# A decoder block on one core: where the pooling's first differences, its weights' splits and some later low parts are made

## The chip, the cores and the metric

One NeuronCore of one Trainium2 chip runs the kernel; the other cores are idle. The metric is the device time of one execution in microseconds, the median of several runs. The engines are named as in the profile: PE is TensorE (PEld its weight loads), DVE is VectorE, ACT is ScalarE, POOL is GpSimd, SP is the engine whose queue issues most DMAs.

## What is computed

One decoder layer on a sequence of 1024 tokens with 1024 channels, in float32. Of it, what matters here (shortened):

```python
h = rms_norm(x, norm_gain) * (1.0 + scale) + shift
q, k, v, z_a, u, z_b, m_a, m_b = split(h @ w_in)           # eight blocks of 1024 columns
p_a = (stick_breaking_attention(q, k, v) * silu(z_a)) @ w_branch_a
# pooling: four groups of 256 channels, trailing windows 2, 4, 8, 16
d = (trailing mean of u over the window) - u               # divided by the available count
pooled = (d @ pool_w[group]) * pool_scale
p_b = (pooled * silu(z_b)) @ w_branch_b
out = x + gate * ((sigmoid(m_a) * p_a + sigmoid(m_b) * p_b) @ w_out)
return rms_norm(out, final_gain)
```

## The kernel before

**Products in two parts.** A float32 operand of a matmul is split into a high part (a cast to the type fp32r, which TensorE takes at full rate) and a low part (the rest, original minus high part). Each product is made from three matmuls: high with high, high with low, low with high (`mm3`, line 152). A matmul has 128 rows of weights and 512 columns. So every weight tile of 128x1024 costs a DMA of 512 KB, a cast and a subtraction of 1024 columns per partition: `split` (line 103) takes the engine of the cast and that of the subtraction as arguments, `load_w` (line 118) loads into the tag `raw` (two buffers, pool `wts`) and splits into the tag `whl` (two buffers).

**Low parts made ahead.** The attention's 40 weight tiles take their low parts from DRAM, except the first eight (`PLAIN`). `make_lo` (line 131) makes them in stages in which there is room: it loads a tile (`l_raw`), ScalarE casts it (`l_hi`), VectorE subtracts in place, and it is stored to `wl_d`. Eight are made beside the product u, fourteen beside v (`LO_V`, 7 in each half), ten after the tiles of pb (`LO_PB`), in program order. Their buffers: three for `l_raw` and one for `l_hi`, in the pool that is open (`vp`, then `pb`).

**Stages, in order.** (1) Loads, norm, modulation, transposition of x into hT, and the product u for the first 512 tokens. (2) u for the rest; its tiles go to DRAM (`u_d`). The weights of u lie in the pool `first`, opened ahead of `init` on the left side of SBUF and closed after v. (3) The values v (lines 353 to 373): 16 tiles of 24 matmuls in two halves; each is emptied from its PSUM bank by a cast on ScalarE and a subtraction on VectorE and stored to `v_d`. (4) The pooling (lines 377 to 425), in pool `pb`: per group of 256 channels two differences, each of a load of u, one to four adds of 1024 columns (tag `win`), a subtraction (`d`, line 397) with two short instructions for its first tokens, and a split into the tag `dhl` (three buffers), all on VectorE; the group's pool weights (`praw`, in the tag `raw` of `wts`; split into `phl`, one buffer); then two output tiles, each with the projection `wzb` (48 matmuls, its weights cast by VectorE and their low part made by GpSimd), the silu of it (lines 409 to 411), twelve matmuls of the pooled tile into the PSUM tag `tr`, and a scaling out of the bank (line 423), a cast and a subtraction into `gb`. (5) pb (lines 428 to 442): gb times w_branch_b, eight weight tiles split by VectorE and GpSimd, with the gate's sum `gacc` beside it. (6) The attention, interleaved with its projections. Its pool `atz` is on the right side of SBUF; `kl` is set to zero by GpSimd at its start (line 460). (7) The attention's output product, the final product and norm.

**What sets the order.** The framework traces the program and then orders each engine's instructions by a simulated timeline, in which an instruction goes as soon as its inputs and its buffer are there, the earlier one in the program first. Only what is pinned keeps its program order: the matmuls and transpositions of stages 1 and 6 and a few loads and casts. In stages 2 to 5 nothing is pinned, so a step can be placed far ahead of or behind its place in the program; what holds it is its inputs and its buffer. The order so planned is fixed on every engine and queue: an instruction whose input is late holds up those behind it. A pool's memory may be that of a closed one; then a tile waits until the tiles that lay there are no longer in use.

Of the kernel before, what the change touches and what calls it, by code (L numbers as in the profile page):

```python
# [9 lines left out]
F32 = mybir.dt.float32  # L10
F32R = mybir.dt.float32r
AF = mybir.ActivationFunctionType
ALU = mybir.AluOpType
PSUM = bass.MemoryType.PSUM

P = 128
D = 1024
# [19 lines left out]
PLAIN = 8  # L37
LO_V = (1, 1, 1, 1, 1, 1, 1, 0)
LO_PB = (1, 1, 1, 1, 1, 1, 2, 2)
HD = 64  # L40

LOAD_WO = (0, 0, 0, 1, 1, 2, 2, 2)
# [8 lines left out]
def block_kernel(ctx, tc, a, out):  # L51
# [3 lines left out]
    def pool(name, **kw):  # L55
        return tc.tile_pool(name=name, bufs=1, reuse_waits="tile", **kw)
# [46 lines left out]
    def split(src, shape, pl, tag, bufs, hi_eng, lo_eng, name):  # L103
        hl = pl.tile([shape[0], 2] + list(shape[1:]), F32R, tag=tag, bufs=bufs, name=name)
        hi, lo = hl[:, 0], hl[:, 1]
        copy_to(hi_eng, hi, src)
        lo_eng.tensor_tensor(lo, src, hi.bitcast(F32), op=ALU.subtract)
        return hi, lo
# [19 lines left out]
    tiles += gates  # L128
    early_lo = iter(range(PLAIN, len(tiles)))

    def make_lo(pl, n):

        for _ in range(n):
            i = next(early_lo)
            raw = pl.tile([P, D], F32, tag="lraw", bufs=3, name=f"l{i}_raw")
            nc.sync.dma_start(raw, a["w_in"][tiles[i]])
            hi = pl.tile([P, D], F32R, tag="lhi", bufs=1, name=f"l{i}_hi")
            act.copy(hi, raw)
            v.tensor_sub(raw.bitcast(F32R), raw, hi.bitcast(F32))
            nc.sync.dma_start(wl_d[i], raw)  # L140
# [27 lines left out]
    def project(ct, name, use, he, le):  # L168
        whl = load_w(a["w_in"][ct], name, he, le)
        for sh in range(2):  # L170
            ps = bank("pj", f"{name}_{sh}")
            mm3(ps, whl, (h_hi, h_lo), range(KB), hmov(sh))
            use(sh, ps)
# [14 lines left out]


    early = ExitStack()  # L190
    first = early.enter_context(pool("first"))
    with pool("init") as init:
        sig = const.tile([P, 8], F32, name="csig")
        act.activation(sig, c_v, AF.Sigmoid)
# [143 lines left out]
            make_h(1, kb, v)  # L338


    with pool("vp") as vp:
        def load_wv(hf, k2):
            raw = wts.tile([P, 2, 512], F32, tag="raw", bufs=2, name=f"wv{hf}_{k2}_raw")
            nc.sync.dma_start(raw.rearrange("p k c -> p (k c)"), a["w_v"][hf, k2])
            return split(raw, [P, 2, 512], vp, "wv", 6, act, v, f"wv{hf}_{k2}")

        wv = [[load_wv(0, k2) for k2 in range(4)]]
        for i in reversed(range(KB)):
            ps = bank("pj", f"u{i}_1")
            mm3(ps, whl[i], h, range(KB), hmov(1))  # L350
            use[i](1, ps)
            make_lo(vp, 1)
        for hf in range(2):
            if hf == 0:
                wv.append([load_wv(1, k2) for k2 in range(4)])
            for sb in range(8):
                ss = slice(sb * P, (sb + 1) * P)
                ps = bank("pj", f"v{sb}_{hf}")
                for kb in range(KB):
                    hh, hl = h_hi[:, kb, ss], h_lo[:, kb, ss]  # L360
                    wh, wl = (w[:, kb % 2] for w in wv[hf][kb // 2])
                    for n, (l, w) in enumerate(((hh, wh), (hh, wl), (hl, wh))):
                        mm(ps, l, w, start=kb == 0 and n == 0, stop=kb == KB - 1 and n == 2)

                vo = vp.tile([P, 8, 2, HD], F32R, tag="vo", bufs=3, name=f"vo{sb}_{hf}")
                pv = ps.rearrange("p (h d) -> p h d", d=HD)
                act.copy(vo[:, :, 0], pv)
                v.tensor_sub(vo[:, :, 1], pv, vo[:, :, 0].bitcast(F32))
                nc.sync.dma_start(
                    v_d[4 * hf:4 * hf + 4, :, sb].rearrange("n p c -> p n c"),  # L370
                    vo.rearrange("p (n h) i d -> p n (h i d)", h=2).bitcast(F32),
                )
                make_lo(vp, LO_V[sb])
    early.close()


    with pool("pb") as pb:
        invn = pb.tile([P, 16], F32, name="invn")
        for j in range(16):
            gp.memset(invn[:, j:j + 1], 1.0 / (16 - j))  # L380
        gb = pb.tile([P, 2, KB, S], F32R, name="gb")
        for g, win in enumerate(WINDOWS):
            dhl = []
            for cb in range(2):
                j = 2 * g + cb
                u = pb.tile([P, S + 16], F32, tag="u", bufs=2, name=f"u{j}")
                v.memset(u[:, S:], 0.0)
                nc.sync.dma_start(u[:, :S], u_d[j])
                cur, n, step = u, S + 16, 1
                while step < win:  # L390
                    nxt = pb.tile([P, S + 16], F32, tag="win", bufs=2, name=f"win{j}_{step}")
                    n -= step
                    v.tensor_add(nxt[:, :n], cur[:, :n], cur[:, step:step + n])  # L393
                    cur, step = nxt, 2 * step
                t0 = S - win + 1
                d = pb.tile([P, S], F32, tag="win", bufs=2, name=f"d{j}")
                v.scalar_tensor_tensor(d[:, :t0], cur[:, :t0], 1.0 / win, u[:, :t0], ALU.mult, ALU.subtract)
                tl = pb.tile([P, 16], F32, tag="tl", bufs=2, name=f"tl{j}")
                v.tensor_mul(tl[:, :win - 1], cur[:, t0:S], invn[:, 16 - win + 1:])
                v.tensor_sub(d[:, t0:], tl[:, :win - 1], u[:, t0:S])  # L400
                dhl.append(split(d, [P, S], pb, "dhl", 3, v, v, f"dhl{j}"))
            praw = wts.tile([P, 2, 256], F32, tag="raw", bufs=2, name=f"praw{g}")
            nc.sync.dma_start(praw, a["pool_w"][g].rearrange("(k p) d -> p k d", p=P))
            ph, pl_ = split(praw, [P, 2, 256], pb, "phl", 1, v, v, f"phl{g}")
            for ob in range(2):
                j = 2 * g + ob
                zs = [pb.tile([P, 512], F32, tag="zs", bufs=3, name=f"zs{j}_{sh}") for sh in range(2)]

                def silu(sh, ps):
                    act.activation(zs[sh], ps, AF.Sigmoid)  # L410
                    v.tensor_mul(zs[sh], ps, zs[sh])  # L411

                project(CZB + j, f"wzb{j}", silu, v, gp)
                for sh in range(2):
                    sl = slice(sh * 512, sh * 512 + 512)
                    ps = bank("tr", f"pool{j}_{sh}")
                    for cb in range(2):
                        (dh, dl) = dhl[cb]
                        oc = slice(ob * P, ob * P + P)
                        for i, (w, m) in enumerate(((ph, dh), (ph, dl), (pl_, dh))):  # L420
                            mm(ps, w[:, cb, oc], m[:, sl], start=cb == 0 and i == 0, stop=cb == 1 and i == 2)
                    z = zs[sh]
                    v.scalar_tensor_tensor(z, ps, psc_v[:, j:j + 1], z, ALU.mult, ALU.mult)
                    act.copy(gb[:, 0, j, sl], z)
                    v.tensor_sub(gb[:, 1, j, sl], z, gb[:, 0, j, sl].bitcast(F32))
        gacc, bg = (pb.tile([P, S + 16], F32, tag="u", bufs=2, name=n)[:, :D] for n in ("gacc", "bg"))
        nc.sync.dma_start(bg, a["b_gate"].broadcast_to([P, D]))
        for j in range(KB):
            sm = [pb.tile([P, 512], F32, tag="zs", bufs=3, name=f"sm{j}_{sh}") for sh in range(2)]
            whl = load_w(a["w_branch_b"][j], f"wb{j}", v, gp)  # L430
            wg = wts.tile([P, D], F32, tag="raw", bufs=2, name=f"wg{j}")
            nc.sync.dma_start(wg, a["w_gate"][j * P:(j + 1) * P, :])
            if j == 0:
                v.tensor_scalar_mul(gacc, wg, sc[:, 0:1])
            else:
                v.scalar_tensor_tensor(gacc, wg, sc[:, j:j + 1], gacc, ALU.mult, ALU.add)
            for sh in range(2):
                ps = bank("pj", f"pb{j}_{sh}")
                mm3(ps, whl, (gb[:, 0], gb[:, 1]), range(KB), hmov(sh))
                act.copy(sm[sh], ps)  # L440
                nc.sync.dma_start(pb_d[j][:, sh * 512:sh * 512 + 512], sm[sh])
            make_lo(pb, LO_PB[j])

        for hf in range(2):
            sl = slice(hf * 512, hf * 512 + 512)
            ps = bank("z", f"gate{hf}")
            mm(ps, ones, gacc[:, sl], start=True, stop=True)
            v.tensor_add(bg[:, sl], ps, bg[:, sl])
        nc.sync.dma_start(g_d, bg[0:1, :])


    logits = ExitStack()
# [394 lines left out]
```

## Time and profile before

| | us |
|---|---|
| median of 3 runs | 1249.1 (1248.1 to 1249.2) |
| the profiled execution, its own time | 1250.9 |
| its span, first to last instruction | 1249.2 |
| PE busy | 1215.2 (97%) |
| DVE busy | 810.5 (65%) |
| ACT busy | 546.3 (44%) |
| POOL busy | 227.6 (18%) |

The chain of work that ended last is 78% PE, 10% DVE, 5% issue and 2% DMA. In the views, a row of the timeline is: start, duration, engine, line, operation, output and input, shapes, count, and in brackets the idle time of the engine before it and what ended it. Rows by stretch give the busy time of PE, PEld, DVE, ACT and POOL with counts, then the granted clock, the DMA engines' share and GB/s. Rows of groups give the count, the busy time in us and the mean in ns, and then the idle time ahead of them. A helper's line stands for all who call it: L107 and L116 are the subtraction and VectorE's cast of a split, L112 is ScalarE's, L92 every matmul.

### The profile page before, as it was taken

Reading aid. Unit: us, or ns where it says so; the run is one execution under the profiler, and the core shown is the slowest. Engines: PE = TensorE matmul, PEld = TensorE weight load, DVE = VectorE, ACT = ScalarE, POOL = GpSimd, SP = SyncE. Lnnn points to the kernel's source line nnn. Section 1 sums busy time; section 2 is a strip of 40 time slices with the busy share of each in tenths; the row PEclk is TensorE's granted clock in tenths of the full one; section 3 lists DMA queues with packets and bytes.
Section 4 is the critical chain, followed back from the end, with each engine's and each line's share of the span. In section 5 each row is a group of like instructions: output and inputs, shape, how many; then the busy total and the mean of one; then the engine's idle time right before and its main releaser. Section 6 shows DMA issues by size and latency. Waiting matters only on the chain.

```text
span 1249.2 us, 16044 instructions
## 1 busy us (share of the span) xinstructions
PE 1215.2 (97%) x5744; PEld 1005.2 (80%) x5744; DVE 810.5 (65%) x1085; ACT 546.3 (44%) x1022; POOL 227.6 (18%) x373
## 2 busy tenths in 40 slices
PE   4999999899999999999999999999999999999998
PEld 3888888688888888888888888888888888888886
DVE  6723452999511168786887877788796864685654
ACT  4654331321111256565566656566565654232101
POOL 2100010111112333221312222132222310001001
PEclk9999999989999999999999999999999999999999
DMA  8649994752344411232322333232233225985612
GB/s 325 265 151 345 320 371 163 274 202 93 118 144 135 151 52 50 69 127 90 105 89 94 114 110 111 73 121 89 89 119 110 74 89 186 352 287 170 201 65 85
DMA packets 72946, 192.97 MB, mean 154 GB/s; under 512 B 7713, under 2 KB 21025, under 8 KB 70946
## 3 DMA queue, kind: packets, MB, share of 16 engines
q1 hardware_dynamic: 62098, 172.80, 40.3%
q10 hardware_dynamic: 10768, 19.14, 4.6%
q8 instruction: 45, 0.74, 0.2%
q14 instruction: 35, 0.29, 0.1%
HBM read 137.38 MB, written 50.34 MB: 150 GB/s over the span
## 4 chain that ended last, share of the span: by engine, by line
PE 78%; DVE 10%; issue 5%; DMA 2%; POOL 1%; ACT 1%; POOLq 0%; SPq 0%; DVEq 0%; ACTq 0%
PE p L92 30%; PE pa L92 7%; PE pb L92 7%; PE v L92 7%; PE o L92 6%; PE av L92 4%; PE z L92 4%; PE u L92 4%; PE wt L92 4%; PE ua L92 2%; DVE om L583 1%; DVE be L584 1%; DMA l_raw<-in_w_in 1%; DVE win L393 1%; PE wzb L92 1%
## 5 line engine op out<-in xcount | busy, mean ns | idle before, releaser
L92 PE MATMUL p<-hT,w 128*128 128x512 f32 x1920 | 534.5, 399 | 0.0
L92 PEld LDWEIGHTS p<-hT,w 128*128 128x128 f32 x1920 | 341.5, 188 | 56.7 <-issue 0.5
L583 DVE TENSOR_TENSOR_SCAN om<-om 128x512 f32<-128x512 f32 (+7 forms) x128 | 175.2, 1368 | 51.7 <-POOL om L581 28.6
L576 ACT ACTIVATE om<-z 128x512 f32<-128x512 f32 (+2 forms) x192 | 94.3, 491 | 104.0 <-PE z L92 101.8
L603 DVE TENSOR_TENSOR wt<-wt,wt 128x512 fp32r<-128x512 f32 (+1 forms) x160 | 101.0, 632 | 47.3 <-ACT wt L602 46.0
L581 POOL TENSOR_SCALAR_AFFINE_SELECT om<-om 128x128 f32<-128x128 f32 x128 | 65.7, 514 | 328.1 <-ACT om L576 301.8
L602 ACT CAST wt<-wt 128x512 fp32r<-128x512 f32 (+1 forms) x160 | 87.3, 546 | 68.7 <-PE wt L92 65.2
L584 DVE TENSOR_TENSOR be<-be,om 128x511 f32<-128x511 f32 (+7 forms) x128 | 99.7, 779 | 10.8 <-ACT wt L602 0.5
L92 PE MATMUL av<-wt,vv 128*128 128x512 f32 x320 | 94.4, 376 | 0.0
L92 PEld LDWEIGHTS wt<-ident,be 128*128 128x128 f32 x576 | 72.0, 140 | 27.5 <-DVE wt L603 3.2
L577 ACT ACTIVATE be<-z 128x512 f32<-128x512 f32 (+2 forms) x192 | 93.6, 487 | 0.0
L92 PE MATMUL wzb<-hT,wzb 128*128 128x512 f32 x384 | 92.9, 398 | 0.1
L92 PE MATMUL wt<-ident,be 128*128 128x128 f32 x576 | 89.2, 273 | 3.8 <-DVE wt L603 3.8
L92 PE MATMUL o<-wo,mhl 128*128 128x512 f32 (+2 forms) x408 | 90.4, 380 | 0.0
L92 PE MATMUL pa<-ga,wa 128*128 128x512 f32 x384 | 89.8, 392 | 0.0
L92 PE MATMUL pb<-gb,wb 128*128 128x512 f32 x384 | 88.1, 391 | 0.0
L92 PEld LDWEIGHTS wzb<-hT,wzb 128*128 128x128 f32 x384 | 73.8, 192 | 16.8 <-DVE zs L411 0.5
L92 PE MATMUL v<-wv,hT 128*128 128x512 f32 x384 | 87.2, 389 | 0.0
L92 PEld LDWEIGHTS o<-wo,mhl 128*128 128x128 f32 x408 | 74.6, 188 | 14.4
L92 PEld LDWEIGHTS pa<-ga,wa 128*128 128x128 f32 x384 | 72.1, 188 | 15.9
L92 PEld LDWEIGHTS pb<-gb,wb 128*128 128x128 f32 x384 | 72.1, 188 | 15.8
L92 PEld LDWEIGHTS v<-wv,hT 128*128 128x128 f32 x384 | 72.1, 188 | 14.9
(121 smaller groups left out, 1458.4 us busy)
## 6 DMA issues: line engine op xcount, KB each, us to landing
w_raw<-in_w_in SPq DMA_DIRECT2D x40, 512.0 KB, 4.3
l_raw<-in_w_in SPq DMA_DIRECT2D x32, 512.0 KB, 5.8
wl_d<-l_raw SPq DMA_DIRECT2D x32, 512.0 KB, 5.3
w<-wl_d SPq DMA_DIRECT2D x32, 512.0 KB, 3.8
v_d<-vo SPq DMA_DIRECT2D x16, 512.0 KB, 5.4
vv<-v_d SPq DMA_DIRECT2D x8, 1024.0 KB, 5.8
wa_raw<-in_w_branch_a SPq DMA_DIRECT2D x16, 512.0 KB, 4.8
wa<-in_w_mod SPq DMA_DIRECT2D x7, 1024.0 KB, 8.7
```

The costliest lines, as they stand in the source:

```text
L92: ins = op(*args, **kw)
L393: v.tensor_add(nxt[:, :n], cur[:, :n], cur[:, step:step + n])
L576: act.activation(om[:, b0:b0 + n], zp[:, :n], AF.Sigmoid, scale=-0.125)
L577: act.activation(be[:, b0:b0 + n], zp[:, :n], AF.Sigmoid, scale=0.125)
L581: gp.affine_select(out=tl[:, :P], in_=tl[:, :P], pattern=[[1, P]], compare_op=ALU.is_gt, fill=fill, base=0, channel_multiplier=-1)
L583: v.tensor_tensor_scan(om[:, :W], om[:, :W], om[:, :W], 1.0, ALU.mult, ALU.min)
L584: v.tensor_mul(be[:, 1:W], be[:, 1:W], om[:, :W - 1])
L602: act.copy(wt[:, 0, :off], pt[:, :off])
L603: v.tensor_sub(wt[:, 1, :off], pt[:, :off], wt[:, 0, :off].bitcast(F32))
```

## The change

- The code of one difference becomes a function, `make_d`, with the same instructions, in a pool `dif` on the right side of SBUF. `dif` is opened after u, where `first` lay, which moves to the right side and is closed there already. The tags `u`, `win`, `tl` and `dhl` are in `dif`; `dhl` has four buffers instead of three.
- `DIFFS = {1: 0, 4: 1}`: differences 0 and 1 (the first group) stand in the program after tiles 1 and 4 of the first half of v. The others stand where they were.
- The pool weights `praw` get a tag of their own in `pb` with two buffers; `phl` has two buffers instead of one.
- The projection wzb is cast by ScalarE, and its low part is made by VectorE (before: VectorE and GpSimd).
- The ten `make_lo` after pb's tiles use buffers of the tag `dhl`, raw tile and cast side by side in one buffer. Those beside u and v are as before.
- `gacc` and `bg` take the tag `u` in `dif`; `dif` is closed after the gate. `invn` is a constant.

```diff
+DIFFS = {1: 0, 4: 1}
...
-    def make_lo(pl, n):
+    def make_lo(pl, n, tag=None):
 
         for _ in range(n):
             i = next(early_lo)
-            raw = pl.tile([P, D], F32, tag="lraw", bufs=3, name=f"l{i}_raw")
+            if tag:
+                both_ = pl.tile([P, 2, D], F32R, tag=tag, bufs=4, name=f"l{i}")
+                raw, hi = both_[:, 0].bitcast(F32), both_[:, 1]
+            else:
+                raw = pl.tile([P, D], F32, tag="lraw", bufs=3, name=f"l{i}_raw")
+                hi = pl.tile([P, D], F32R, tag="lhi", bufs=1, name=f"l{i}_hi")
             nc.sync.dma_start(raw, a["w_in"][tiles[i]])
-            hi = pl.tile([P, D], F32R, tag="lhi", bufs=1, name=f"l{i}_hi")
             act.copy(hi, raw)
             v.tensor_sub(raw.bitcast(F32R), raw, hi.bitcast(F32))
             nc.sync.dma_start(wl_d[i], raw)
...
-    first = early.enter_context(pool("first"))
+    first = early.enter_context(pool("first", side="right"))
...
+    def make_d(j):
+        win = WINDOWS[j // 2]
+        u = dif.tile([P, S + 16], F32, tag="u", bufs=2, name=f"u{j}")
+        v.memset(u[:, S:], 0.0)
+        nc.sync.dma_start(u[:, :S], u_d[j])
+        cur, n, step = u, S + 16, 1
+        while step < win:
+            nxt = dif.tile([P, S + 16], F32, tag="win", bufs=2, name=f"win{j}_{step}")
+            n -= step
+            v.tensor_add(nxt[:, :n], cur[:, :n], cur[:, step:step + n])
+            cur, step = nxt, 2 * step
+        t0 = S - win + 1
+        d = dif.tile([P, S], F32, tag="win", bufs=2, name=f"d{j}")
+        v.scalar_tensor_tensor(d[:, :t0], cur[:, :t0], 1.0 / win, u[:, :t0], ALU.mult, ALU.subtract)
...
+        dhls[j] = split(d, [P, S], dif, "dhl", 4, v, v, f"dhl{j}")
...
             use[i](1, ps)
             make_lo(vp, 1)
+        early.close()
+        diffs = ExitStack()
+        dif = diffs.enter_context(pool("dif", side="right"))
...
                 make_lo(vp, LO_V[sb])
-    early.close()
+                if 8 * hf + sb in DIFFS:
+                    make_d(DIFFS[8 * hf + sb])
...
-            praw = wts.tile([P, 2, 256], F32, tag="raw", bufs=2, name=f"praw{g}")
+            for j in (2 * g, 2 * g + 1):
+                if j not in dhls:
+                    make_d(j)
+            dhl = [dhls.pop(2 * g), dhls.pop(2 * g + 1)]
+            praw = pb.tile([P, 2, 256], F32, tag="praw", bufs=2, name=f"praw{g}")
             nc.sync.dma_start(praw, a["pool_w"][g].rearrange("(k p) d -> p k d", p=P))
-            ph, pl_ = split(praw, [P, 2, 256], pb, "phl", 1, v, v, f"phl{g}")
+            ph, pl_ = split(praw, [P, 2, 256], pb, "phl", 2, v, v, f"phl{g}")
...
-                project(CZB + j, f"wzb{j}", silu, v, gp)
+                project(CZB + j, f"wzb{j}", silu, act, v)
...
-        gacc, bg = (pb.tile([P, S + 16], F32, tag="u", bufs=2, name=n)[:, :D] for n in ("gacc", "bg"))
+        gacc, bg = (dif.tile([P, S + 16], F32, tag="u", bufs=2, name=n)[:, :D] for n in ("gacc", "bg"))
...
-            make_lo(pb, LO_PB[j])
+            make_lo(dif, LO_PB[j], "dhl")
...
+    diffs.close()
```

More of the change, by code (lines that the diff above doesn't have):

```diff
@@ L338, in block_kernel @@
             make_h(1, kb, v)
+    invn = const.tile([P, 16], F32, name="invn")
+    for j in range(16):
+        gp.memset(invn[:, j:j + 1], 1.0 / (16 - j))
+    dhls = {}
+    def make_d(j):
[12 more added lines that the diff above has]
+        v.scalar_tensor_tensor(d[:, :t0], cur[:, :t0], 1.0 / win, u[:, :t0], ALU.mult, ALU.subtract)
+        tl = dif.tile([P, 16], F32, tag="tl", bufs=2, name=f"tl{j}")
+        v.tensor_mul(tl[:, :win - 1], cur[:, t0:S], invn[:, 16 - win + 1:])
+        v.tensor_sub(d[:, t0:], tl[:, :win - 1], u[:, t0:S])
+        dhls[j] = split(d, [P, S], dif, "dhl", 4, v, v, f"dhl{j}")
     with pool("vp") as vp:
@@ L373, in block_kernel @@
                 make_lo(vp, LO_V[sb])
-    early.close()
+                if 8 * hf + sb in DIFFS:
+                    make_d(DIFFS[8 * hf + sb])
     with pool("pb") as pb:
-        invn = pb.tile([P, 16], F32, name="invn")
-        for j in range(16):
-            gp.memset(invn[:, j:j + 1], 1.0 / (16 - j))
         gb = pb.tile([P, 2, KB, S], F32R, name="gb")
         for g, win in enumerate(WINDOWS):
[L383 to L401, printed above, removed]
-            praw = wts.tile([P, 2, 256], F32, tag="raw", bufs=2, name=f"praw{g}")
+            for j in (2 * g, 2 * g + 1):
[3 more added lines that the diff above has]
+            praw = pb.tile([P, 2, 256], F32, tag="praw", bufs=2, name=f"praw{g}")
             nc.sync.dma_start(praw, a["pool_w"][g].rearrange("(k p) d -> p k d", p=P))
-            ph, pl_ = split(praw, [P, 2, 256], pb, "phl", 1, v, v, f"phl{g}")
+            ph, pl_ = split(praw, [P, 2, 256], pb, "phl", 2, v, v, f"phl{g}")
             for ob in range(2):
```

## The prediction

> **What bounds the kernel now.** I read the page first: the span, then the slices of TensorE, VectorE and the granted clock.
>
> ```profile
> span 1249.2 us, 16044 instructions
> PE   4999999899999999999999999999999999999998
> DVE  6723452999511168786887877788796864685654
> PEclk9999999989999999999999999999999999999999
> ```
>
> A slice is 31.2 us. TensorE is full almost everywhere, so only a place where it isn't can give time back. Between the loads at the start and the tail there is one such place, around slice 8, and there VectorE stands at 9 for three slices. Second view: busy time by stage (the values' product v, the pooling with its gate projection wzb, the pooling's output product pb).
>
> ```profile
> core 0: us, PE busy (x) PEld busy (x) DVE busy (x) ACT busy (x) POOL busy (x), PEclk, DMA share, GB/s
> 122.00:209.50 87.50, 87.50 (x388) 72.48 (x387) 33.49 (x35) 26.83 (x33) 5.27 (x18) 1.00 0.81 287
> 209.50:330.20 120.70, 114.34 (x481) 92.74 (x480) 109.88 (x142) 28.44 (x41) 19.64 (x8) 0.96 0.55 183
> 330.20:418.10 87.90, 87.90 (x385) 72.12 (x385) 14.28 (x16) 11.00 (x18) 18.24 (x8) 1.00 0.38 129
> ```
>
> In pb a matmul takes 87.90 / 385 = 0.2283 us. The pooling's 481 at that pace take 109.8 us, and they took 120.7: **10.9 us are lost there**, and that is the ceiling of what a repair of this stage can give. Its VectorE is busy for 91%, while in v and pb it has 54 and 74 us free. Third view: where inside the stage.
>
> ```profile
> 239.60:242.85 3.25, 0.00 (x1) 0.00 (x1) 3.22 (x8) 0.22 (x2) 0.00 (x0) 0.94 0.98 353
> 242.85:247.30 4.45, 4.41 (x12) 3.23 (x12) 4.45 (x6) 3.03 (x5) 0.00 (x0) 0.66 0.92 307
> 247.30:250.30 3.00, 0.03 (x1) 0.03 (x1) 3.00 (x5) 1.89 (x3) 0.00 (x0) 0.83 0.20 82
> 250.30:260.30 10.00, 10.00 (x32) 7.98 (x33) 8.90 (x14) 2.51 (x3) 0.00 (x0) 0.71 0.76 237
> ```
>
> Two gaps, 3.25 + 3.00 us. After each the granted clock is down, and the matmuls cost more than 0.2283 us: 4.45 - 12 x 0.2283 = 1.7 and 10.00 - 32 x 0.2283 = 2.7. Together 10.65 of the 10.9, so the loss is these two gaps with their slow clock, about 2.2 us of clock for each. Last view: the timeline around them.
>
> ```profile
> 235.77 3.25 POOL L107 TENSOR_TENSOR wzb<-wzb_raw,wzb 128x1024 fp32r<-128x1024 f32 x1 [10.07 <-DVE wzb L116]
> 236.69 3.42 DVE L397 SCALAR_TENSOR_TENSOR d<-win,u 128x1021 f32<-128x1021 f32 x1
> ...
> 242.05 0.75 DVE L423 SCALAR_TENSOR_TENSOR zs<-pool,vecs,zs 128x512 f32<-128x512 f32 x1
> 242.85 4.42 PE L92 MATMUL pool<-dhl,phl 128*128 128x512 f32 x12 [3.25 <-DVE u L387]
> 249.80 0.42 DVE L116 CAST phl<-praw 128x512 fp32r<-128x512 f32 x1
> 250.27 1.22 PE L92 MATMUL pool<-dhl,phl 128*128 128x512 f32 x2 [3.01 <-DVE phl L116]
> ```
>
> The first gap ends when L423 has emptied a PSUM bank of the first pooled tile (the row names the memset beside it, which has no reader in TensorE). L423 stood in VectorE's queue behind a difference that took 3.42 us while GpSimd made a low part. The second ends with the cast of the second group's pool weights into phl, which has one buffer and so can't be filled before the first group's matmuls are over. So: VectorE's queue, and one buffer.
>
> **The change part by part.** Groups of VectorE's instructions in the pooling stage, then GpSimd's and ScalarE's there, and the tile dhl (min/median/max ns):
>
> ```profile
> L107 DVE TENSOR_TENSOR dhl<-d,dhl 128x1024 fp32r<-128x1024 f32 x8 | 15.3, 1909 | 0.0
> L139 DVE TENSOR_TENSOR l_raw<-l_raw,l_hi 128x1024 fp32r<-128x1024 f32 x10 | 12.2, 1218 | 1.8 <-ACT l_hi L138 1.8
> L393 DVE TENSOR_TENSOR win<-win 128x1037 f32<-128x1037 f32 x6 | 10.2, 1698 | 0.1
> L393 DVE TENSOR_TENSOR win<-u 128x1039 f32<-128x1039 f32 x8 | 9.9, 1235 | 0.1
> L116 DVE CAST dhl<-d 128x1024 fp32r<-128x1024 f32 x8 | 5.5, 687 | 0.0
> L397 DVE SCALAR_TENSOR_TENSOR d<-win,u 128x1021 f32<-128x1021 f32 x2 | 4.6, 2316 | 0.0
> L116 DVE CAST wzb<-wzb_raw 128x1024 fp32r<-128x1024 f32 x6 | 4.1, 685 | 0.3 <-DMA wzb_raw<-in_w_in 0.3
> L107 DVE TENSOR_TENSOR phl<-praw,phl 128x512 fp32r<-128x512 f32 x4 | 2.7, 683 | 0.0
> L397 DVE SCALAR_TENSOR_TENSOR d<-win,u 128x1023 f32<-128x1023 f32 x2 | 2.4, 1218 | 0.0
> ...
> L107 POOL TENSOR_TENSOR wzb<-wzb_raw,wzb 128x1024 fp32r<-128x1024 f32 x6 | 16.2, 2697 | 105.0 <-DVE wzb L116 105.0
> ...
> L138 ACT CAST l_hi<-l_raw 128x1024 fp32r<-128x1024 f32 x10 | 10.5, 1051 | 30.6 <-DMA l_raw<-in_w_in 25.4 <-DVE l_raw L139 5.2
> ...
> L107 DVE TENSOR_TENSOR dhl<-d,dhl x8: 1210/1220/3102, 223.7 to 317.7; 128x1024 fp32r<-128x1024 f32 x8
> ```
>
> *Two differences move into v.* One of window 2 is an add 1.24, a subtract 1.22, a cast 0.69 and a low part 1.22: 4.4 us (the tail's two short instructions left out). VectorE's stage loses 2 x 4.4 = 8.7, and v's 54 free us take them. With four dhl buffers, open from the end of u, the planner may pull the next two forward as well.
>
> *wzb's splits.* The casts leave VectorE (-4.1) for ScalarE (6 x 1.05 = 6.3 on its 28.4 busy of 120.7; behind them queue the sigmoids that empty wzb's banks). The low parts come from GpSimd to VectorE: 6 x 1.22 = +7.3.
>
> *GpSimd is silent.* What VectorE paid beside it: dhl 15.3 - 8 x 1.22 = 5.5, win 10.2 - 6 x 1.235 = 2.8, d 4.6 - 2 x 1.22 = 2.2, together -10.5.
>
> A rule speaks against this part: the Trainium skill, Perfetto Trace Analysis, section Optimizing Scalar/DVE Operations, says that work may be taken off a saturated VectorE, onto ScalarE or even GpSimd, while the change puts work of GpSimd on it; it adds that the two share a read port, so that this might not help. By the first half alone the sum lacks the -10.5; the trace, with 3.42 us beside GpSimd against 1.22, bears out the second half.
>
> *The ten low parts of later weights* (make_lo after pb) use dhl's buffers instead of their own. In the pooling they cost VectorE 12.2. Now they get a buffer before the differences need it (in v) or after (end of the pooling, pb): between 0 and 12.2 leave. In pb, VectorE and ScalarE work 14.3 and 11.0 us of 87.9, so 12.2 and 10.5 more are covered; the loads stand in SP's queue ahead of wb's.
>
> *Sum for VectorE:* 109.9 - 8.7 - 4.1 + 7.3 - 10.5 = 93.9, less up to 12.2: between 82 and 94 against TensorE's 109.8. It is at the limit no longer.
>
> *praw and phl get two buffers each, of their own.* The second group's cast is then free of the first group's matmuls, and wzb's loads no longer share buffers with praw. But praw now lies where v's buffers were: that is the first rival.
>
> *Waits added.* In v the window adds wait for u's load, and the subtractions that empty v's banks queue behind them. A tile of v is 24 matmuls, 24 x 0.2283 = 5.5 us, with a second bank beside it, so a wait below 5.5 us costs nothing. The attention's right-hand tiles (kl first) now lie over the differences' pool, whose gacc and bg live until the gate is stored:
>
> ```profile
> 422.45 3.94 POOL L460 MEMSET kl<- 64x1024 f32 x4
> ...
> 441.89 0.39 PE L92 MATMUL z<-kl,q 128*128 128x512 f32 x1
> ```
>
> kl is ready at 426.4 and read at 441.9: 15 us hide a later memset. I cost it at nothing.
>
> Of the 10.9 us I take back both gaps and their clock but for a rest of 1.8, since VectorE still fills some 80% of the stage and empties every bank of it: **9.1 us**. The profiled execution took 1250.9 us with a span of 1249.2, the runs' median is 1249.1; I take the saving from the median: **1240.0 us**. The bound below: all 10.9 back, and 1.7 for an attention whose planned order may shift either way: 1236.5.
>
> **The rivals.** *A new gap at the stage's head.*
>
> ```profile
> 210.88 3.24 DMA v_d<-vo
> ...
> praw<-in_pool_w SPq DMA_DIRECT2D x4, 256.0 KB, 4.2
> ```
>
> Before, the first praw lay ready long ahead in a weight buffer. If its new place is under v's last output tile, it is loaded from 214.1 on, lands at 218.3, and is split (0.42 + 0.68) by 219.4. wzb's first tile (48 matmuls, 11.0 us) covers until 220.5. But if the planner, which trusts its own DMA times, puts pooled matmuls after half of it, at 215.0, TensorE waits 4.4 and loses 2.2 of clock: 1246.6 at worst, 1244 typically.
>
> *VectorE still sets the pace.* If GpSimd's silence gives nothing and the ten low parts stay in the stage, its sum is 109.9 - 8.7 - 4.1 + 7.3 = 104.4 and the stage shrinks by those 5.5: 1243.6. This is what the skill's rule would make of it. Against it stands the 3.42.
>
> *Slower: the low parts are pulled into v and fill the DMA engines.*
>
> ```profile
> 170.00:180.00 10.00, 10.00 (x46) 8.29 (x45) 3.94 (x4) 2.23 (x3) 2.40 (x1) 1.00 1.01 361
> ...
> 190.00:200.00 10.00, 10.00 (x46) 8.29 (x45) 1.38 (x2) 1.17 (x2) 0.00 (x0) 1.00 0.31 107
> 200.00:210.00 10.00, 10.00 (x45) 8.27 (x45) 0.69 (x1) 1.05 (x2) 0.00 (x0) 1.00 0.31 106
> ```
>
> Mid-v the transfers are at their limit (361 GB/s, share 1.01); only the last 20 us are free, 20 x 0.69 = 13.8. Ten low parts read and write 10 x 1.05 MB, at 361 GB/s 29 us. ScalarE casts them in the same queue in which it empties v's banks, so if all ten are placed inside v, v waits for 29 - 13.8 = 15 us: 1255. It decides from some eight low parts on (more than 13.8 + 9.1 us of transfer). Against: the planner times transfers too, and v ran full beside a saturated DMA.
>
> *No change:* both gaps come back elsewhere (banks emptied late by ScalarE's longer queue, wb late behind the low parts on SP): 1249.
>
> **How the numbers follow.** About 0.2%, 2.5 us, is what a measurement here can tell from no change. Forecast 0.60; gap at the head 0.16; VectorE's pace 0.08; no change 0.09; slower by the DMA in v 0.07. Faster is the first three, 0.84; same 0.09; slower 0.07. The range takes the same three: 1236.5 to 1246.6.
>
> **What would show it.** Right: the pooling stage at 110 to 113 us, no gap of 3 us and clock 1.00 in it, GpSimd empty there but for wb, dhl's low parts at 1.22 each, VectorE's busy time at 82 to 94, two or more differences inside v with v still at 87.5. Wrong: a wait of a pooled matmul for phl or praw at the stage's head; VectorE above 100 us; v longer than 88.5 with ScalarE waiting for l loads; a stage after pb that lengthens.

## The result and the profile after

| | before | after |
|---|---|---|
| median of the runs taken side by side, us | 1248.8 (1248.1 to 1249.2) | 1235.9 (1235.1 to 1237.1) |
| ratio, 95% interval | | 0.9903 (0.9891 to 0.9915) |
| the profiled execution, its own time | 1250.9 | 1235.3 |
| its span | 1249.2 | 1233.5 |

The kernel is faster by 13.0 us. The forecast was 1240.0; the median lies 4.1 us below it and 0.6 below the lower end of the range.

First the page of the kernel after: span, and the slices of TensorE, VectorE and the granted clock.

```profile
span 1233.5 us, 16052 instructions
PE   5999999999999999999999999999999999999997
DVE  6723873695510298786878878688786863685654
PEclk8999999999999999999999999999999999999999
```

TensorE's 8 in slice 8 is gone, and so is the dip of the clock after it. VectorE stood at 4, 5, 2, 9, 9, 9, 5, 1 in slices 5 to 12 and now stands at 8, 7, 3, 6, 9, 5, 5, 1: work went from the pooling into v. Then the stages (v, pooling, pb), with the columns of the prediction's second view:

```profile
120.90:207.94 87.04, 87.04 (x385) 72.07 (x385) 57.77 (x74) 28.35 (x35) 0.00 (x0) 1.00 0.92 335
207.94:316.74 108.80, 108.80 (x481) 90.09 (x481) 72.70 (x97) 29.80 (x43) 2.80 (x2) 1.00 0.35 118
316.74:403.79 87.05, 87.05 (x385) 72.08 (x385) 21.64 (x22) 15.72 (x23) 18.74 (x8) 1.00 0.54 189
```

In the pooling TensorE is busy for all 108.80 us at clock 1.00; VectorE's 110 us there are 72.7. By the chain of waits, which gives each stage's first matmul (before, v began at 122.46, the pooling at 209.51, pb at 330.40 and its last matmul ended at 418.30), the 15.6 us between the two profiled executions lie so: pooling 120.9 to 108.8, **12.1 us**; pb 87.90 to 87.05, 0.85; the last products behind the attention 1.2; and 1.6 ahead of v, where TensorE waited for its first load 12.0 us in one execution and 10.4 in the other. TensorE waited for that load between 9.8 and 12.2 us in the profiled executions of all kernels below, whatever was changed, so the 1.6 belongs to no kernel. v took 87.05 and 87.04, the attention 648.0 both times. The medians are 13.0 apart, not 15.6: the profiled execution of before lies 2.1 above its median, a little more than its late load explains, and that of after 0.6 below. So without the load the pair still overstates the gain by some 1 us, and the 12.1 of the pooling is the figure of one execution: two runs below that keep both gaps (64 bytes moved, nothing else) took 119.0 and 119.4 us for that stage instead of 120.9.

The planner did more than the change wrote. The tile dhl (its splits; min/median/max ns, first and last start) and, of the later low parts, the tile l:

```profile
L109 DVE TENSOR_TENSOR dhl<-d,dhl x8: 1206/1216/1226, 133.2 to 275.3; 128x1024 fp32r<-128x1024 f32 x8
```

```profile
L143 SPq DMA_DIRECT2D l<-in_w_in x10: 328/330/966, 288.9 to 327.7; - x10
L145 DVE TENSOR_TENSOR l<-l x10: 1221/1225/2355, 293.5 to 335.0; 128x1024 fp32r<-128x1024 f32 x10
```

The splits of the differences start at 132 and the first four are complete before the pooling begins at 207.94, not two. The ten low parts, which took VectorE 9.7 us in the first 50 us of the pooling before, are loaded only from 288.9 on, when the differences have let go of their buffers.

### The profile page after: what moved, and what is told of

Read it like the earlier page. It is cut to its first block, busy times and chain, and to the rows that moved or that the text cites. A ratio compares the mean times of both kernels' runs of the same rounds, so it can differ in the third digit from the quotient of the medians.

```text
span 1233.5 us, 16052 instructions
## 1 busy us (share of the span) xinstructions
PE 1209.5 (98%) x5744; PEld 1005.2 (81%) x5744; DVE 807.5 (65%) x1085; ACT 554.1 (45%) x1030; POOL 206.0 (17%) x365
## 4 chain that ended last, share of the span: by engine, by line
PE 84%; issue 6%; DVE 5%; POOL 2%; ACT 0%; POOLq 0%; DVEq 0%; ACTq 0%
PE p L94 29%; PE pb L94 7%; PE pa L94 7%; PE v L94 7%; PE wzb L94 7%; PE o L94 6%; PE u L94 4%; PE av L94 4%; PE wt L94 4%; PE z L94 4%; PE ua L94 2%; PE pool L94 2%; DVE om L601 2%; DVE be L602 2%; POOL om L599 1%
## 5 line engine op out<-in xcount | busy, mean ns | idle before, releaser
L94 PE MATMUL wzb<-hT,wzb 128*128 128x512 f32 x384 | 88.5, 389 | 0.0
L94 PEld LDWEIGHTS o<-wo,mhl 128*128 128x128 f32 x408 | 74.6, 188 | 14.1
```

Source lines behind the costliest of these rows:

```text
L94: ins = op(*args, **kw)
```

## The experiments

The theories, as they are named in the expectations. **A**: VectorE had more to do in the pooling than fits, and phl's single buffer made the second gap (the prediction's). **B**: GpSimd slowed VectorE, and its silence is the gain. **C**: the buffers of praw and phl are. **D**, formed after the first four runs: the ten low parts, which stood at the stage's head because their buffers were free there, made both gaps. "Before" in a ratio is the kernel before, run on the same chip beside it.

### Which of the small parts matter

**The splits of wzb go back to VectorE and GpSimd**, in the kernel after:

```diff
-                project(CZB + j, f"wzb{j}", silu, act, v)
+                project(CZB + j, f"wzb{j}", silu, v, gp)
```

> The changed kernel, with wzb's splits as before (cast on VectorE, low part on GpSimd). Theory A (both gaps came from VectorE's overfull queue and phl's single buffer): VectorE's 72.7 us in the pooling become 72.7 - 7.3 + 4.1 + up to 10.5 = 80 of 108.8, still far from full, so no gap of 3 us comes back and the time is 1236 to 1238. Rival B (it was chiefly VectorE's instructions slowed beside GpSimd): at least one gap with its slow clock comes back, 5 us or more, 1241 or above. Rival C (it was the buffers of praw and phl alone): 1236.

1236.15 us, 0.9905 (0.9889 to 0.9922): all of the gain is still there. The pooling:

```profile
209.52:318.32 108.80, 108.80 (x482) 90.09 (x481) 72.72 (x96) 24.16 (x37) 17.73 (x7) 1.00 0.34 116
```

GpSimd works 17.7 us here, and TensorE waits for nothing. VectorE does pay for it: with the casts of wzb in place of the subtractions its sum should be 72.7 + 4.1 - 7.3 = 69.5 us, and it is 72.7. Two of its groups in the kernel after, then the same two here:

```profile
L361 DVE TENSOR_TENSOR win<-win 128x1037 f32<-128x1037 f32 x3 | 3.7, 1233 | 0.0
L118 DVE CAST dhl<-d 128x1024 fp32r<-128x1024 f32 x4 | 2.8, 688 | 0.0
```

```profile
L361 DVE TENSOR_TENSOR win<-win 128x1037 f32<-128x1037 f32 x3 | 5.5, 1838 | 0.0
L118 DVE CAST dhl<-d 128x1024 fp32r<-128x1024 f32 x4 | 4.9, 1218 | 0.0
```

So GpSimd still slows VectorE by some 3 us, and nothing comes of it in the stage's time. As the cause of the gain B falls.

**One buffer for phl, and praw in the weights' buffers again**, in the kernel after:

```diff
-            praw = pb.tile([P, 2, 256], F32, tag="praw", bufs=2, name=f"praw{g}")
+            praw = wts.tile([P, 2, 256], F32, tag="raw", bufs=2, name=f"praw{g}")
...
-            ph, pl_ = split(praw, [P, 2, 256], pb, "phl", 2, v, v, f"phl{g}")
+            ph, pl_ = split(praw, [P, 2, 256], pb, "phl", 1, v, v, f"phl{g}")
```

> The changed kernel, with praw in the weights' tag raw and phl with one buffer, as before. A: the gap at the second group comes back, some 3 us and 2 of clock, 1239 to 1242. B: 1236, no gap. C: all that was gained in the pooling goes, 1246 or above.

1236.87 us, 0.9912 (0.9897 to 0.9927), with a pooling of 108.80 us and no wait in it:

```profile
209.71:318.51 108.80, 108.80 (x481) 90.12 (x481) 72.95 (x97) 29.99 (x43) 3.06 (x2) 1.00 0.35 123
```

C falls, and A missed too (it expected 1239 to 1242): phl's one buffer doesn't make the second gap by itself, since it holds up nobody once VectorE comes in time. Whether the added buffers would have closed the second gap in the kernel before was not tried.

**The kernel before with wzb split by ScalarE and VectorE** and nothing else of the change:

```diff
-                project(CZB + j, f"wzb{j}", silu, v, gp)
+                project(CZB + j, f"wzb{j}", silu, act, v)
```

> The kernel before, with only wzb's splits changed (cast on ScalarE, low part on VectorE, none on GpSimd). VectorE's sum in the pooling is 109.9 - 4.1 + 7.3 - 10.5 = 102.6. A: the first gap shrinks or goes, the second (phl's buffer) stays, 3 to 5 us gained, 1244 to 1246. B: both gaps go, 1240 or below. C: 1249.

1247.37 us, 0.9996 (0.9987 to 1.0006): no change that can be told. A expected 1244 to 1246 and B 1240 or below, and both missed. VectorE's sum in the stage went from 110.0 to 105.4, but the gaps stay. The waits of TensorE:

```profile
PE pool L92 <- DVE phl L116: 3.4, 1, 3.4
PE pool L92 <- DVE zs L423: 1.9, 2, 1.6
PE wzb L92 <- DVE zs L411: 0.7, 1, 0.7
```

The same two places wait for the same engine, with GpSimd out of it.

### The differences in v

**`dif` opened only after v, no `DIFFS`**, in the kernel after:

```diff
-        diffs = ExitStack()
-        dif = diffs.enter_context(pool("dif", side="right"))
...
-                if 8 * hf + sb in DIFFS:
-                    make_d(DIFFS[8 * hf + sb])
...
+    diffs = ExitStack()
+    dif = diffs.enter_context(pool("dif", side="right"))
```

> The changed kernel, with the differences' pool opened after v instead of after u, so that no difference can be made in v. Four whole differences and most of a fifth (2 x 4.4 + 2 x 5.6 + about 5 = 25 us) come back to VectorE, 98 of 108.8. A: the first pooled matmuls wait again and 1 to 6 us are lost, 1237 to 1242. B and C: 1236.

1235.61 us, 0.9903 (0.9888 to 0.9917). This run doesn't tell what it was made for: since `dif` lies in free memory on the right side, the planner moved four differences into v all the same (the first at 128.9). It does tell that the places written in v aren't needed.

**The same with `dif` on the left**, over v's own memory, so that no difference can start before v ends:

```diff
+    dif = diffs.enter_context(pool("dif"))
```

> The changed kernel, with the differences' pool over v's memory, so that no difference can start before v ends (opening it later on the right did not keep them out of v). The splits, the four dhl buffers, praw's and phl's buffers and the low parts' place stay. VectorE's 72.7 us in the pooling become 98 of 108.8. A: a wait for the first differences and 1 to 6 us lost, 1237 to 1242. D: no gap but perhaps a short one at the very head, 1236 to 1237.

1238.61 us, 0.9923 (0.9909 to 0.9936). The pooling has 95.2 us of VectorE in it and no wait that the profile lists:

```profile
208.19:317.80 109.61, 109.47 (x481) 90.17 (x481) 95.22 (x133) 28.49 (x41) 2.41 (x1) 1.00 0.39 132
```

The time lies in A's range, but not for A's reason: of the 2.7 us that it is slower than the kernel after, 2.2 are in pb, which took 89.23 instead of 87.05 (below). So moving differences into v gave nothing by itself either, with the low parts out of the way.

### The low parts

**The kernel before with the ten low parts in dhl's three buffers**, which is the change's line for them alone:

```diff
... (make_lo with its tag, as in the change)
-            make_lo(pb, LO_PB[j])
+            make_lo(pb, LO_PB[j], "dhl")
```

> The kernel before, with only the ten low parts after pb made in the differences' three dhl buffers, so that they come after the differences. VectorE's sum in the pooling is 109.9 - 12.2 = 97.7 and more, the DMA engines are free at the stage's head. Theory A (the sum over VectorE's whole stage decides, and phl's buffer makes the second gap): the first gap shrinks as it did with the splits changed, the second stays, 1242 to 1246. Theory D (the ten low parts at the stage's head, in VectorE's and ScalarE's queues and on the DMA engines, make both gaps): both go, 1236 to 1239.

1240.23 us, 0.9935 (0.9920 to 0.9950). This line alone takes both gaps away, just above the 1239 of D's range and below A's 1242. GpSimd still splits, phl has one buffer and no difference is in v. The pooling, up to the first matmul of pb, and TensorE's waits in it and in pb:

```profile
207.95:317.97 110.02, 109.43 (x482) 89.88 (x481) 97.25 (x131) 19.98 (x32) 20.46 (x7) 1.00 0.38 129
```

```profile
PE pb L92 <- ACT sm L444: 1.3, 1, 1.3
PE pb L92 <- DVE zs L415: 1.0, 1, 1.0
PE wzb L92 <- DVE zs L415: 0.6, 1, 0.6
```

The clock is 1.00, VectorE works 97.25 us, and TensorE waits 0.6 us in the pooling. What is left are the two waits of 1.0 and 1.3 at the head of pb, where the low parts (loaded from 295 on) now meet the last pooled tiles.

**The kernel after with the ten low parts first in the pooling's program**, still in dhl's buffers:

```diff
         gb = pb.tile([P, 2, KB, S], F32R, name="gb")
+        make_lo(dif, sum(LO_PB), "dhl")
...
-            make_lo(dif, LO_PB[j], "dhl")
```

> The changed kernel, with the ten low parts in the program ahead of the pooling, in the same dhl buffers: they are made in v and at the pooling's head, ahead of differences 2 to 7. A: VectorE's sum in the pooling rises by less than 12 us to some 85 of 108.8, no gap, 1236 to 1237. D: the gaps at the head come back in part, 3 to 8 us, 1239 to 1244. Third (the prediction's slower rival): v is stretched by its full DMA engines, 1245 or above, with v above 90 us.

1247.01 us, 0.9994 (0.9985 to 1.0003): the gain is gone, and more than D expected (1239 to 1244). But the trace shows another way to it than in the kernel before:

```profile
PE wzb L94 <- DVE zs L429: 6.4, 1, 6.4
PE pool L94 <- DVE phl L118: 1.5, 1, 1.5
```

```profile
L144 ACT CAST l<-l 128x1024 fp32r<-128x1024 f32 x4 | 4.1, 1044 | 8.7 <-DMA l<-in_w_in 8.7
```

The second row is ScalarE's group of the low parts' casts between 209.82 and 240: ScalarE sat idle for 8.7 us ahead of them, waiting for their loads, with its silu and wzb's cast queued behind. VectorE idled too (6.82 us for wzb's cast, 6.72 us for that of l). So this run shows a queue held up by a late load. It looks like support for D and says little on VectorE's work.

### What the low parts do there

**The kernel after with the low parts' own buffers**, so that they stand at the pooling's head as before; phl, praw and dhl's three buffers as before too:

```diff
... (dhl with three buffers, phl with one, praw in the tag raw)
-            make_lo(dif, LO_PB[j], "dhl")
+            make_lo(pb, LO_PB[j])
```

> The change, but with the weights' low parts of the branch product in buffers of their own again (three for the raw tile, one for its cast), so that they are free from the end of v and stand at the head of the pooling as in before; one buffer for the pooled weights, three for the differences, as in before. The differences still start in v, GpSimd has no split, VectorE has no cast of the weights. Theory A (VectorE has too much to do in the stage): its sum there is 94 to 97 us as in the change with no difference in v (95.2, no gap), so no gap: 1236 to 1239. Theory D (it is where the ten low parts stand): the gaps come back in part, 3 to 10 us: 1240 to 1246.

1235.51 us, 0.9901 (0.9887 to 0.9914): no gap, level with the kernel after. D in its simple form falls: all ten low parts are made in the first 50 us of the stage, and nobody waits.

**The kernel before with the DMAs of the ten low parts alone**, no cast and no subtraction (the last ten weight tiles of the attention's projections get the whole weight for a low part; the expectation calls them the output stage's):

```diff
-            act.copy(hi, raw)
-            v.tensor_sub(raw.bitcast(F32R), raw, hi.bitcast(F32))
+            if work:
+                act.copy(hi, raw)
+                v.tensor_sub(raw.bitcast(F32R), raw, hi.bitcast(F32))
...
-            make_lo(pb, LO_PB[j])
+            make_lo(pb, LO_PB[j], False)
```

> The kernel before, with the ten low parts of the branch product's stage reduced to their two DMAs: loaded and stored, with no cast and no subtraction, so the last ten weight tiles of the output stage get the whole weight in place of its low part. Theory D by the queues (ScalarE's and VectorE's work of the low parts stands ahead of what the pooling needs): the gaps are gone, 1238 to 1241, VectorE's sum in the stage 97 to 99. D by the DMA engines (the low parts' 5 MB each way hold up the differences' rows and the pooled weights): the gaps stay, 1245 to 1249. Theory A by the sum: 97 to 99 is close to the 95 that had none, 1238 to 1242.

1240.18 us, 0.9937 (0.9922 to 0.9952). One wait of 1.9 us is left in the stage.

**The kernel before with their cast and subtraction alone**, computed from a tile of h, no DMAs (the last ten tiles read another tile's low part):

```diff
-            nc.sync.dma_start(raw, a["w_in"][tiles[i]])
+            if dmas:
+                nc.sync.dma_start(raw, a["w_in"][tiles[i]])
+            src = raw if dmas else h_hi[:, 0].bitcast(F32)
... (cast and subtraction read src; no store without dmas)
-            make_lo(pb, LO_PB[j])
+            make_lo(pb, LO_PB[j], False)
```

> The kernel before, with the ten low parts' cast and subtraction kept in the same buffers, but their DMAs left out: they are computed from a tile of h that lies in SBUF, and the last ten weight tiles of the output stage read another tile's low part. Theory D by the queues: gaps remain, 1244 to 1249. D by the DMA engines: no gaps, 1237 to 1241. Theory A (VectorE's sum stays at 110): gaps remain, 1246 to 1249.

1248.76 us, 1.0006 (0.9997 to 1.0015): TensorE waits 6.1 us in the pooling again, by other last links than before (2.9 and 1.7 us for a VectorE step on zs, 0.8 for one on dhl). So it is the low parts' work in the queues, not their transfers. Both this run and the one before it came out as D by the queues expected, and as A expected by the stage's sum.

In the kernel before it is VectorE's queue that is late, rather than ScalarE's, which has the casts. In the 25 us around the gaps VectorE is idle for 0.3 us, and five low parts take 6.1 us of it (VectorE, ScalarE, clock, DMA share, GB/s in the second row):

```profile
234.50:259.50 25.00, 18.74 (x63) 14.42 (x62) 24.66 (x33) 8.26 (x12) 3.25 (x1) 0.80 0.71 235
```

```profile
234.50:259.50 25.00, 6.07 (x5) 4.78 (x6) 0.80 0.71 235
```

And with the low parts' own buffers in the kernel after, ScalarE casts all ten there and works more than in the kernel before (21.1 us against 14.1 in the first 50), and nobody waits. The first 50 us of the pooling in five kernels say how (columns as in the prediction's second view). The kernel before, the time of its low parts in it (columns of that row: VectorE, ScalarE, clock, DMA share, GB/s), and then the same two for the run without DMAs:

```profile
209.50:259.50 50.00, 43.74 (x173) 35.01 (x172) 44.78 (x60) 14.10 (x19) 5.66 (x2) 0.90 0.76 256
```

```profile
209.50:259.50 50.00, 9.73 (x8) 8.45 (x9) 0.90 0.76 256
```

```profile
208.59:258.59 50.00, 43.89 (x170) 34.08 (x169) 45.31 (x58) 16.33 (x20) 6.53 (x2) 0.90 0.30 100
```

```profile
208.59:258.59 50.00, 12.13 (x10) 0.00 (x0) 0.90 0.30 100
```

Then the low parts out (in dhl's buffers), and their DMAs alone:

```profile
207.95:257.95 50.00, 49.41 (x218) 40.37 (x217) 45.09 (x64) 7.79 (x13) 8.98 (x3) 1.00 0.36 123
```

```profile
208.22:258.22 50.00, 48.08 (x211) 39.25 (x211) 45.27 (x66) 7.80 (x14) 6.87 (x3) 1.00 0.89 326
```

Then the low parts at the head, but with differences in v:

```profile
207.31:257.31 50.00, 50.00 (x222) 41.40 (x222) 36.56 (x47) 21.08 (x27) 0.00 (x0) 1.00 0.79 275
```

Without low parts, VectorE does some 45 us of work in these 50 and TensorE loses 0.6 to 1.9 us. With them it is busy for the same 45 us, but 10 to 12 of those went to low parts, and as much of what the pooling needed came later: TensorE loses 6 us and the clock drops to 0.90. Where the low parts (12.2 us in this stretch too) stand beside differences that have left for v, VectorE has 36.6 and TensorE loses nothing. The DMA share of 0.89 in the run with the DMAs alone costs at most those 1.9 us.

So the last form of the theory is A made local: **with the low parts, VectorE has some 55 to 57 us of work for the first 50** (an estimate: those 45 and the 10 to 12), and what the pooling waits for comes late. This form is argued. No run was made to test it, and the 45 us are what VectorE did there, some of it perhaps ahead of need. Nor does any run separate it from a limit on the stage's sum: VectorE has 72.5 to 73.0, 84.9, 95.2, 97.25 and 98.5 us in the pooling of the kernels that wait at most 1.9 us there, and 105.4 to 110.5 in those that wait 6 to 7. For the local form speaks that the stage's sum doesn't give the size: 105.4 us would fit into TensorE's 108.8 and 110.0 is 1.2 too much, yet both wait 6 us, and where they wait VectorE is full. The run with the low parts first in the program, with 87.1 us and 8.2 of waiting, fits neither: there a load came late.

Two parts of the change each take the gaps away, and it makes both: the low parts' move, shown alone, and the differences in v, shown only together with wzb's other splits, which did nothing alone.

### The last two microseconds: pb and pa

The products with the branch weights, pb in its stage and pa behind the attention, take less time after, with nothing waiting before or after. Groups of the kernel before, then of the kernel after:

```profile
L92 PE MATMUL pa<-ga,wa 128*128 128x512 f32 x384 | 89.8, 392 | 0.0
L92 PE MATMUL pb<-gb,wb 128*128 128x512 f32 x384 | 88.1, 391 | 0.0
```

```profile
L94 PE MATMUL pa<-ga,wa 128*128 128x512 f32 x384 | 88.8, 389 | 0.0
L94 PE MATMUL pb<-gb,wb 128*128 128x512 f32 x384 | 87.2, 389 | 0.0
```

From one start to the next it is 229 ns before and 227 after. A candidate is where the tiles lie: the change makes `invn` (64 bytes in each partition) a constant. By the order of the pools in the program (no view shows addresses) that shifts the weights' buffers by 64 bytes, and gb, ahead of which it stood, not at all.

**The kernel before with 64 unused bytes among the constants**, which shifts the weights and gb alike:

```diff
+    pad = const.tile([P, 16], F32, name="pad")
+    gp.memset(pad, 0.0)
```

> The kernel before, with one more constant of 64 bytes a partition ahead of all weight and activation tiles (as the change's moved invn makes it) and one more memset at the start. If the place of the tiles in SBUF sets the matmul's step (229 ns in pb and pa before, 227 after), pb and pa are at 227 here and the time is 1246 to 1247; if not, 229 and no change.

1247.05 us, 0.9992 (0.9983 to 1.0001); one of the two products follows:

```profile
L94 PE MATMUL pa<-ga,wa 128*128 128x512 f32 x384 | 88.8, 389 | 0.0
L94 PE MATMUL pb<-gb,wb 128*128 128x512 f32 x384 | 88.1, 391 | 0.0
```

**The kernel before with invn moved to the constants**, as in the change, and nothing else of it:

```diff
+    invn = const.tile([P, 16], F32, name="invn")
...
-        invn = pb.tile([P, 16], F32, name="invn")
```

> The kernel before, with one thing moved: the 64-byte table of reciprocals (invn) lies among the constants, as in the change, and no longer ahead of gb. That shifts the weights' buffers by 64 bytes and takes away the 64 bytes by which gb stood off. If the matmuls' step depends on where the two operands lie against each other, pb and pa both go from 229 to 227 ns (pb 384 matmuls 88.1 to 87.2, pa 384 matmuls 89.8 to 88.8 us), the two gaps of the pooling stay, and the time is 1.9 us below before: 1246.5 to 1247.5, ratio 0.998 to 0.999. If the rest of the gain (pb and pa together 2.0 us) came from the lighter stage before and after instead, both stay at 229 ns and the time is before's, 1248.8.

1245.80 us, 0.9985 (0.9977 to 0.9994):

```profile
L92 PE MATMUL pa<-ga,wa 128*128 128x512 f32 x384 | 88.8, 389 | 0.0
L92 PE MATMUL pb<-gb,wb 128*128 128x512 f32 x384 | 87.2, 389 | 0.0
```

pa is faster in both runs, pb only where the weights moved against gb. The two gaps of the pooling are there in both. So 64 bytes of placement give some 2 us, and it is not the place of one operand alone. The run with `dif` on the left, where gb lies elsewhere again, has 395 ns for pb (232 from start to start), 2.2 us more than the kernel after in that stage. Which rule of the addresses this follows stays open; it wasn't tried.

## Why the prediction was right, and where it was wrong

**What bounds: right, and the ceiling was too low.** The one place that gave time back is the pooling, through its two gaps and their clock. The ceiling of 10.9 us took pb's 0.2283 us as TensorE's pace; that stage itself ran slow by its placement. At 108.80 us for the same matmuls the loss was 12.1 us, and all of it came back. The rest of 1.8 that I kept for "VectorE still fills some 80% of the stage" was nothing. The term of 9.1 was 12.1 in the profiled pair and, by the medians, 11.1 (13.0 less the 1.9 of pb and pa). That makes 2 to 3 of the 4.1 us by which the forecast was high. Most of the others are those 1.9 us, which no step of the prediction saw: it put the move of invn at nothing and gave no reason.

**VectorE's queue as the cause of the gaps: right.** The run with the low parts' casts and subtractions but no DMAs keeps the waits, the run with their DMAs alone all but loses them. The second half of that step, "and one buffer", failed: phl with one buffer makes no gap in the kernel after, and none in the kernel before with the low parts out.

**GpSimd is silent, -10.5: wrong as a term of the gain.** The dearest term of the sum bought nothing: after with GpSimd at work has the gain whole, before without GpSimd has none of it. What it priced did come. In before with the other splits the three groups of VectorE take 5.5, 2.8 and 2.2 us less, as the sum has it:

```profile
L107 DVE TENSOR_TENSOR dhl<-d,dhl 128x1024 fp32r<-128x1024 f32 x8 | 9.8, 1219 | 0.0
L393 DVE TENSOR_TENSOR win<-win 128x1037 f32<-128x1037 f32 x6 | 7.4, 1234 | 0.0
L397 DVE SCALAR_TENSOR_TENSOR d<-win,u 128x1021 f32<-128x1021 f32 x2 | 2.4, 1218 | 0.0
L400 DVE TENSOR_TENSOR d<-tl,u 128x15 f32<-128x15 f32 x2 | 2.2, 1096 | 0.0
```

VectorE's time in the stage fell by 4.6 (110.0 to 105.4) and not by the 7.3 that -10.5, -4.1 and +7.3 make, since a short subtraction now met GpSimd's split of wb (the last row, 0.3 us in the kernel before). The step that failed is the next one, from VectorE's sum to the gaps: the cheaper instructions didn't bring forward what TensorE waited for. The rule of the Trainium skill that was weighed here (Perfetto Trace Analysis, section Optimizing Scalar/DVE Operations: work may be taken off a saturated VectorE onto GpSimd, though a shared port may spoil it) is neither borne out nor refuted by the time: with GpSimd's splits or without, the kernel after takes 1236. Its second half, that the shared port may spoil it, agrees with VectorE's slower instructions beside GpSimd (casts of dhl at 1218 ns in the mean against 688, window adds at 1838 against 1233).

**Two differences move into v, -8.7: larger, and not needed alone.** Four moved, as the text allowed for, and v kept its 87.04 us with the DMA engines at a share of 0.92. With the low parts out of the pooling's first half, they can stay where they were; with the low parts there, they and the other splits make the room.

**The low parts, "between 0 and 12.2": the step that was mis-sized by being left open.** It is the one term that does the whole repair alone, as one line in the kernel before. The text added it to a sum over the stage and used only "82 to 94 against 109.8". By the stage's sum, half of the low parts even come back (five of them, 6.1 us), at its end, where nobody misses VectorE. What went away is their work in the first 50 us, 9.7 us.

**The sum for VectorE, 82 to 94:** measured 72.7, since four differences and part of a fifth left instead of two, and five of the low parts with them; it no longer limits anything, as was said.

**The rivals.** There is no gap at the head: no pooled matmul waits. VectorE doesn't set the pace. The low parts were not pulled into v, so the slower case with its full DMA engines didn't come; in the run where they come first in the program, v's DMA share was 0.97 and v 87.27 us, still no stretch of it. The slower case that the runs did show is another one: low parts in dhl's buffers ahead of the differences hold up the queues in the pooling and undo the gain.

## What to carry to other kernels

When an engine seems overfull, add up its work over the stretch in which its results are waited for as well as over the stage: here VectorE was busy for 91% of the stage and for 24.66 of the 25 us around the gaps, and 6.1 of those were work that nobody needed before the end of the next stage. Work without a near deadline takes its place in the queue from when its buffer is free, so the buffer that it shares decides when it runs. Of a change with several edits, take each out alone: here the other splits and the added buffers gave nothing that could be told, two parts did the same thing twice, and the move of a 64-byte constant gave 2 us.

## What the runs showed of the hardware that was not expected

The step of a 128x512 matmul changed with the place of its tiles in SBUF, by a shift of 64 bytes in two cases: 227, 229 or 232 ns from start to start (389, 391 to 392, 395 ns in the groups) in products with the same shapes, types and clock, worth 0.9 to 2.2 us for 384 of them.

The gaps cost more than themselves, and short ones did not: TensorE lost 6 us in the first 50 where the granted clock fell to 0.90, while the wait of 1.9 us in the run with the DMAs alone left it at 1.00. The price varies: with 6.2 us of waiting the stage of the kernel before was 12.1 us longer than after, with 6.7 and 7.0 us of it (64 bytes moved) 10.2 and 10.6.

Beside GpSimd's splits the low parts of dhl took up to 3102 ns in the kernel before and at most 1224 ns in the kernel after with GpSimd's splits back. There other instructions met them, casts and a window add, for some 3 us in all: what GpSimd costs VectorE depends on the order, and not only on whether both are in the stage.

The matmuls of 128x512 in fp32r took 389 ns each in v, one every 227 ns at clock 1.00, and the four in plain float32 behind pb (the gate's) 592 ns.
